# An encoder layer in split float32: residual rows and middle activations kept in DRAM during the FFN, token sums packed, splitting queued part by part

## The chip, the core and the metric

The kernel runs on one core of a Trainium2 chip. The metric is the device time of one execution in microseconds, lower is better; a median of several runs is given, with their lowest and highest. The profile and the trace come from one profiled execution.

The engines are called TensorE (PE in the profile; PEld is its weight load), VectorE (DVE), ScalarE (ACT), GpSimd (POOL) and SyncE (SP). Each works through its own queue in order; semaphores tie the queues together. SyncE's and GpSimd's queues also issue DMAs.

## What is computed

One layer of a bidirectional encoder on 256 tokens with 2048 features, all float32: a layer norm, one input projection, two kinds of attention, an output projection, and then the part that this change touches, a gated feed-forward network of width 5632 between two layer norms.

```python
h = layer_norm(x, ln_in_g, ln_in_b)
proj = einsum('bsd,de->bse', h, w_in)            # ... two attentions -> mixed inputs
mixed = einsum('bse,ed->bsd', concatenate([na_out, diff_out], -1), w_out)
h = layer_norm(ALPHA * h + mixed, ln1_g, ln1_b)
ffn = einsum('bsf,fd->bsd', silu(h @ w_gate) * (h @ w_up), w_down)
h = layer_norm(ALPHA * h + ffn, ln2_g, ln2_b)
```

## The kernel before

**Split products.** Every large product is made of three matmuls on operands in the format fp32r. A float32 matrix is split into a high half (`hi`, a rounding copy, made by ScalarE) and a low half (`lo`, the rest, a subtraction made by VectorE); the product is hi*hi + hi*lo + lo*hi. Weights are split on chip: `load` (line 326) brings a unit, 128 rows by 1024 columns, to `raw[u]` through SyncE's queue; `split_hi` and `split_lo` make `wh[u]` and `wl[u]`.

**Slots.** Nearly all large tiles come from one pool, `slab`, of 46 slots of 4 KB per partition (`slot`, line 262). A new tile takes a slot whose last tenant is done; if its last reader has not finished, the instruction that fills the slot waits. Residual rows `h` (4 slots) live there from the start to the end, the split transposed FFN input `h1T` (8) and the token sums `forms` (8) through the gate/up stage, and the finished middle activations as `mid_whole` (one per 512 columns, 11 in all) from their making to the down projection.

**Units and stages.** `units` lists the weight units in the order of work: w_in, w_out, then one group of 512 columns of gate and up (`f`, units `FFN` to `SG`), then five slices j of 1024 columns, each with 16 gate units and 16 up units (`SG` to `SE`), then the down projection in two halves of 44 units.

**Fast products.** In the five slices two units make a pair: a 2x2 block of weights against a 2x2 block of tokens. Even pairs (`SEVEN`) are done with seven products instead of eight, which needs sums of weight blocks (`seven_parts`, line 891: sums on VectorE, then their splits on both engines) and sums of token blocks (`more_forms`, line 508: four per pair). Odd pairs take eight plain products with two token differences (line 508 too). `take_product` (line 975) issues the three matmuls of a product into one of eight PSUM banks and, after a product's last pair, the operations that combine the products: a copy on ScalarE, then sums on VectorE, and `block_end` (line 1011) with the activation function or the product of gate and up. Of the up half each finished 128x512 block is transposed on TensorE and copied by ScalarE into `mid_whole` (`mid_side`, line 866); `mid_split` (line 874) splits it for the down projection.

**What sets the order.** Instructions are written out in an order found while the program is built. `Timed` (line 60) keeps a model clock for each engine. The loop at line 1254 goes through the TensorE steps; before each it loads units up to `NPRE` or, for products, `NPRE_S` ahead, forces the splits of the next `URGENT` steps, lets `side` tasks (transposes, norms, attention) go where the model has room, and queues splitting work for steps up to `AHEAD` or `AHEAD_S` ahead. For a seven-product pair that work is a list of five stages, each with operations of both engines, and a stage goes out only if both engines' clocks are at most `SPARE` (2 us) beyond TensorE's:

```python
for p in coming:
    todo = prepare(*p)
    while todo and nc.ready(*todo[0][0]) <= now and max(nc.clock["act"], nc.clock["dve"]) <= now + SPARE:
        todo.pop(0)[1]()
    if todo:
        break
```

The model knows when a tile in a ring or a bank is reused, but not when a slot of the slab is.

Of the kernel before, what the change touches and what calls it, by code (L numbers as in the profile page):

```python
# [15 lines left out]
P = 128  # L16
# [18 lines left out]
URGENT = 3  # L35
NSG = 5
SEVEN = (0, 2, 4, 6)


class Engine:  # L40
# [6 lines left out]
    def __getattr__(self, op):  # L47
        def call(*args, **kw):
            result = getattr(self.engine, op)(*args, **kw)  # L49
            outs, ins = [], []  # L50
            for i, (key, x) in enumerate([("", x) for x in args] + list(kw.items())):
                if hasattr(x, "tensor") and hasattr(x, "ap"):
                    (outs if key in ("out", "accum_out") or (i == 0 and not key) else ins).append(x)
            self.timed.note(self.name, op, outs, ins)
            return result

        return call
# [187 lines left out]
def layer_kernel(ctx: ExitStack, tc: tile.TileContext, A: dict, out: bass.AP):  # L245
# [5 lines left out]
    tmp = ctx.enter_context(tc.tile_pool(name="tmp", bufs=2))  # L251
    slab = ctx.enter_context(tc.tile_pool(name="slab", bufs=46))
    dram = ctx.enter_context(tc.tile_pool(name="dram", bufs=1, space=bass.MemoryType.DRAM))
# [4 lines left out]
    def nm(s):  # L258
        uid[0] += 1
        return f"{s}_{uid[0]}"  # L260

    def slot(shape, dt=F32):
        return slab.tile(shape, dt, tag="slab", name=nm("sl"))

# [78 lines left out]

    def split(u):
        if u not in wh:
            split_hi(u)
            split_lo(u)

    acc = {}

    def mm_step(t, u):
# [5 lines left out]
        xh = xh[:, t * P : (t + 1) * P]  # L357
        xl = xl[:, t * P : (t + 1) * P]
# [7 lines left out]
        nc.tensor.matmul(a1, xl, hi[:, 512:], start=False, stop=sp)  # L366

    def mm_step32(t, u, lhs):
# [19 lines left out]
    AHEAD = 7  # L388
    AHEAD_S = 13
    NPRE = 7  # L390
    NPRE_S = 5

# [54 lines left out]
    def ln_side(key, t, g, b, store, tiles, n_whole):  # L447
# [10 lines left out]
        for c in range(4):  # L458
# [46 lines left out]

    hF, forms = {}, {}

    def more_forms(i):
# [16 lines left out]
        f = f[:, :n]  # L525
        parts = slot([P, 2, n, P], F32R)
        yield "act", [f]
# [346 lines left out]
    def mid_split(c):  # L874

        if c not in mid_tiles:
            side.drain_until(lambda: have.get(("mid whole", c), 0) == 2)
            new_T(mid, mid_tiles, c)
            hi, lo = mid_tiles[c]
            nc.scalar.activation(hi, mid_whole[c], AF.Copy)  # L880
            nc.vector.tensor_tensor(lo, mid_whole[c], hi.bitcast(F32), op=ALU.subtract)
            have["mid", c, 0] = have["mid", c, 1] = 1

# [5 lines left out]
    sums = {}  # L889

    def seven_parts(u):

        r1, r2 = raw[u], raw[u + 1]

        def one():
            sums[u] = dict(b11=slot([P, 2, 512], F32R), t=[slot([P, 2, 512]), slot([P, 2, 512])])
            nc.scalar.activation(sums[u]["b11"][:, 0], r1[:, :512], AF.Copy)
            nc.vector.tensor_tensor(sums[u]["t"][0][:, 0], r1[:, :512], r1[:, 512:], op=ALU.add)

        def two():  # L900
            split_hi(u + 1)
            s = sums[u]
            nc.vector.tensor_tensor(s["t"][0][:, 1], r1[:, 512:], r2[:, 512:], op=ALU.add)
            nc.vector.tensor_tensor(s["b11"][:, 1], r1[:, :512], s["b11"][:, 0].bitcast(F32), op=ALU.subtract)

        def three():
            split_lo(u + 1)
            s = sums[u]
            s["hi"] = [slot([P, 2, 512], F32R), slot([P, 2, 512], F32R)]
            s["lo"] = [slot([P, 2, 512], F32R), slot([P, 2, 512], F32R)]  # L910
            nc.scalar.activation(s["hi"][0], s["t"][0], AF.Copy)

        def four():
            s = sums[u]
            a, b = s["t"]
            nc.vector.tensor_tensor(b[:, 0], a[:, 0], r2[:, 512:], op=ALU.add)
            nc.vector.tensor_tensor(b[:, 1], b[:, 0], r2[:, :512], op=ALU.add)
            nc.scalar.activation(s["hi"][1], b, AF.Copy)
            nc.vector.tensor_tensor(s["lo"][0], a, s["hi"][0].bitcast(F32), op=ALU.subtract)

        def five():
            s = sums[u]
            nc.vector.tensor_tensor(s["lo"][1], s["t"][1], s["hi"][1].bitcast(F32), op=ALU.subtract)

        return [([r1], one), ([r1, r2], two), ([r2], three), ([r2], four), ([r2], five)]

# [4 lines left out]
    def products(u):  # L931
# [12 lines left out]

        def t(n, m):
            return lambda: (sums[u]["hi"][n][:, m], sums[u]["lo"][n][:, m])

        a_, b_, c_, d_ = x(0, 0), x(1, 0), x(0, 1), x(1, 1)
        if i in SEVEN:
            def b11():  # L950
                return sums[u]["b11"][:, 0], sums[u]["b11"][:, 1]

            return [
                (1, a_, b11),
                (2, b_, b(1, 0)),
                (3, f(2), b(1, 1)),
                (5, f(3), t(0, 0)),
                (7, f(0), t(0, 1)),
                (6, f(1), t(1, 0)),
                (4, d_, t(1, 1)),  # L960
            ]
# [13 lines left out]
    def take_product(u, n):  # L975
# [10 lines left out]
        nc.tensor.matmul(q[m], xh, yl, start=False, stop=False)  # L986
        nc.tensor.matmul(q[m], xl, yh, start=False, stop=stop)
        if not any(x in left for x in (1, 6, 7)) and 1 in q:
# [4 lines left out]
            nc.vector.tensor_tensor(vw[:, 0], q[7], e[:, 1], op=ALU.add)  # L993
            part["q1"], part["v"], part["vw"], part["w"] = e[:, 0], e[:, 1], vw[:, 0], vw[:, 1]
            for x in (1, 6, 7):
# [11 lines left out]
        elif stop and m == 4:  # L1007
            block_end(name, 1, 0, q[4], part["vw"], ALU.subtract)
            banks.give(q.pop(4))

# [152 lines left out]
    def last_steps():  # L1163
# [6 lines left out]
        for i, a in enumerate(acc[1]):  # L1170
            cols = slice(i * 512, i * 512 + 512)
            for u in us:
                xh, xl = (x[:, P:] for x in mid[units[u]["k"]])
                nc.tensor.matmul(a, xh, wh[u][:, cols], start=False, stop=False)
# [10 lines left out]
    def prepare(u, seven):  # L1185

        if u not in stages:
            if seven:
                stages[u] = seven_parts(u)
            else:  # L1190
                stages[u] = [([raw[u]], lambda: split(u))]
                if units[u]["group"][0] == "d" and isinstance(units[u]["group"], tuple):
                    c = units[u]["k"] // 4
                    if c not in mid_tiles:
                        stages[u].insert(0, ([], lambda: mid_split(c)))
        return stages[u]

    class Step:
# [24 lines left out]
        def finish_parts(self):  # L1223
            for p in self.parts:
                todo = prepare(*p)
                while todo:
                    todo.pop(0)[1]()

        def operands(self):
# [8 lines left out]
            t = self.t  # L1238
            return [wh[self.u], wl[self.u], *(x[:, t * P : (t + 1) * P] for x in un["lhs"][un["k"]])]

# [13 lines left out]
    for i, step in enumerate(order):  # L1254
# [5 lines left out]
        for _ in range(8):  # L1260
            now = nc.clock["pe"]
            side.elementwise(now, BACKLOG)
            for p in coming:
                todo = prepare(*p)
                while todo and nc.ready(*todo[0][0]) <= now and max(nc.clock["act"], nc.clock["dve"]) <= now + SPARE:
                    todo.pop(0)[1]()
                if todo:
                    break
            task, when = side.best()
# [51 lines left out]
```

## Time and profile before

| | us |
|---|---|
| median of 3 runs | 1149.44 |
| lowest, highest | 1146.36, 1149.57 |
| profiled execution, its own time | 1151.8 |
| its span, first to last instruction | 1150.0 |

| engine | busy us | share of the span |
|---|---|---|
| TensorE, matmuls | 1128.6 | 98% |
| TensorE, weight loads | 914.2 | 79% |
| VectorE | 855.2 | 74% |
| ScalarE | 572.3 | 50% |
| GpSimd | 43.2 | 4% |

How to read it: an instruction of the trace has a start and an end on its engine; idle time before it is put down to the instruction that released it last. All operations are recorded under one line (L49, a helper), so groups are told apart by their tiles: `sl` is any tile of the slab, `acc` a PSUM bank, `s`, `o` and `nb` are rings of small tiles, `ident` the matrix for transposes. In a table of stretches the columns are: length, then busy time and count of PE, PEld, DVE, ACT and POOL, the granted clock of TensorE as a share, the DMA engines' busy share, GB/s. The FFN starts near 405 us, the five slices run from about 463 to 904, the down projection from there to 1138.

### The profile page before, as it was taken

To read this page: it belongs to the slowest core of one execution; us is meant where nothing else is said; L and a number is where in the kernel's file an instruction comes from. 1 tells how busy PE (TensorE), PEld (TensorE's weight loads), DVE (VectorE), ACT (ScalarE), POOL (GpSimd) and SP (SyncE) were. 2 spreads that over 40 slices of the span, in tenths; PEclk is the share of its full clock that TensorE was granted. 3 is DMA by queue.
4 is the path that set the end of the run, shared out by engine and by line. 5 is a ranking of instruction groups with operands and counts; after the bars stand their busy time and mean duration, and the time that the engine had idled before them with its cause. 6 is when DMAs were issued, how large, how long until landed. Compare 5 with 4: busy or idle time off the path is not lost.

```text
span 1150.0 us, 13909 instructions
## 1 busy us (share of the span) xinstructions
PE 1128.6 (98%) x5064; PEld 914.2 (79%) x5064; DVE 855.2 (74%) x1110; ACT 572.3 (50%) x740; POOL 43.2 (4%) x81
## 2 busy tenths in 40 slices
PE   9999999999999999999999999999999999999997
PEld 4788888888888858888778778778778888888885
DVE  7863866447784399989999989999989855455535
ACT  5552655426572155654654654555556544434420
POOL 2000002111000000000000000000000000000001
PEclk9999999999999999999999999999999999999999
DMA  9864548796676623656555556465556755577621
GB/s 329 268 187 151 154 148 184 189 216 157 163 255 204 235 91 115 213 187 203 195 185 196 170 188 234 128 220 183 170 196 223 269 194 174 177 232 246 217 79 73
DMA packets 64053, 218.51 MB, mean 190 GB/s; under 512 B 7669, under 2 KB 7797, under 8 KB 63985
## 3 DMA queue, kind: packets, MB, share of 16 engines
q1 hardware_dynamic: 61056, 209.74, 54.3%
q0 software_dynamic: 2768, 7.81, 5.0%
q8 instruction: 39, 0.64, 0.2%
q14 instruction: 30, 0.24, 0.1%
q10 hardware_dynamic: 160, 0.08, 0.0%
HBM read 215.50 MB, written 2.11 MB: 189 GB/s over the span
## 4 chain that ended last, share of the span: by engine, by line
PE 78%; DVE 13%; issue 3%; ACT 3%; DMA 1%; POOL 1%; POOLq 0%; ACTq 0%; DVEq 0%
PE acc L49 78%; DVE sl L49 10%; ACT sl L49 3%; DVE s L49 1%; DVE o L49 1%; ACT s L49 0%; DMA ident<-in_c_ident_dram 0%; DMA sl<-in_w_gate_dram 0%; DMA sl<-in_w_up_dram 0%; DVE stats L49 0%; POOL rstd L49 0%; POOL rs L49 0%; ACT o L49 0%; ACT L49 0%; POOLq L1317 0%
## 5 line engine op out<-in xcount | busy, mean ns | idle before, releaser
L49 PE MATMUL acc<-sl,sl 128*128 128x512 f32 (+1 forms) x4712 | 1076.7, 389 | 12.2 <-DVE o L49 5.5
L49 PEld LDWEIGHTS acc<-sl,sl 128*128 128x128 f32 x4712 | 869.5, 189 | 200.5 <-DVE sl L49 10.8
L49 DVE TENSOR_TENSOR sl<-sl,sl 128x1024 fp32r<-128x1024 f32 (+2 forms) x611 | 628.7, 1073 | 124.9 <-ACT sl L49 96.6
L49 ACT ACTIVATE sl<-sl 128x1024 fp32r<-128x1024 f32 (+1 forms) x491 | 473.2, 1011 | 297.1 <-DVE sl L49 167.5
L49 ACT ACTIVATE sl<-acc 128x256 fp32r<-128x256 f32 (+2 forms) x70 | 33.0, 499 | 102.4 <-PE acc L49 89.7
L49 DVE TENSOR_TENSOR sl<-acc,sl 128x256 fp32r<-128x256 f32 (+2 forms) x92 | 53.2, 593 | 33.4 <-ACT sl L49 32.6
L49 ACT COPY sl<-acc 128x512 f32<-128x512 f32 x50 | 28.2, 586 | 77.5 <-PE acc L49 77.4
L49 DVE SCALAR_TENSOR_TENSOR sl<-sl,acc 128x512 f32<-128x512 f32 x16 | 10.9, 679 | 58.1 <-PE acc L49 58.1
L49 DVE TENSOR_SCALAR sl<-acc 128x512 f32<-128x512 f32 x8 | 5.5, 688 | 37.2 <-PE acc L49 37.2
L49 DVE TENSOR_TENSOR sl<-sl 128x512 f32<-128x512 f32 x40 | 27.3, 683 | 0.0
L49 POOL DMA_DIRECT2D sl<-in_ln_g_dram x4 | 2.2, 560 | 652.2 <-DMA sl<-in_w_down_dram 596.7
L49 POOL DMA_DIRECT2D nb<-in_na_rpb_dram x32 | 19.6, 620 | 87.5 <-DVE s L49 87.5
L49 ACT ACTIVATE s<-s 128x512 f32<-128x512 f32 x20 | 12.3, 633 | 20.6 <-DVE s L49 20.6
L49 ACT ACTIVATE s<-s,mx 128x256 f32<-128x256 f32 x32 | 15.9, 500 | 12.5 <-DVE mx L49 12.5
L49 PEld LDWEIGHTS acc<-ident,s 128*128 128x128 f32 x136 | 17.1, 145 | 4.7 <-DVE o L49 0.9
L49 PE MATMUL acc<-ident,s 128*128 128x128 f32 x136 | 20.7, 281 | 0.1
L49 PEld LDWEIGHTS acc<-ident,sl 128*128 128x128 f32 x128 | 15.0, 140 | 7.0 <-issue 3.2
L49 DVE SCALAR_TENSOR_TENSOR sl<-sl,rstd,sl 128x512 f32<-128x512 f32 x22 | 16.5, 751 | 4.0 <-POOL rstd L49 3.1
L49 DVE BATCH_NORM_STATS2 stats<-sl 128x6 f32<-128x512 f32 x24 | 16.3, 690 | 3.0 <-DMA sl<-in_x_dram 2.4
L49 DVE SCALAR_TENSOR_TENSOR sl<-sl,mv,sl 128x512 f32<-128x512 f32 x24 | 17.7, 746 | 0.3
L49 PE MATMUL acc<-ident,sl 128*128 128x128 f32 x128 | 17.6, 273 | 0.1
L49 ACT ACTIVATE rows<-ident,rstd 128x128 f32<-128x128 f32 x1 | 0.4, 402 | 34.3 <-POOL rstd L49 34.3
(74 smaller groups left out, 198.9 us busy)
## 6 DMA issues: line engine op xcount, KB each, us to landing
sl<-in_w_in_dram SPq DMA_DIRECT2D x96, 512.0 KB, 4.9
sl<-in_w_down_dram SPq DMA_DIRECT2D x88, 512.0 KB, 4.3
sl<-in_w_gate_dram SPq DMA_DIRECT2D x80, 512.0 KB, 4.0
sl<-in_w_up_dram SPq DMA_DIRECT2D x80, 512.0 KB, 4.3
sl<-in_w_out_dram SPq DMA_DIRECT2D x32, 512.0 KB, 5.4
sl<-in_w_gate_dram SPq DMA_DIRECT2D x16, 256.0 KB, 4.0
sl<-in_w_up_dram SPq DMA_DIRECT2D x16, 256.0 KB, 4.2
sl<-in_x_dram SPq DMA_DIRECT2D x8, 256.0 KB, 5.0
```

Of the source, the lines that this page charges most:

```text
L49: result = getattr(self.engine, op)(*args, **kw)
```

## The change

It has three parts.

First, tiles leave the slab during the FFN. The residual rows are written to DRAM (`h_d`) by GpSimd's queue as they are transposed and read back by SyncE's queue ten units before the second half of the down projection. Finished middle activations are copied to a ring of two tiles, written to DRAM (`mid_d`) by GpSimd's queue, and read back chunk by chunk by SyncE's queue when the down projection's units are loaded. The token sums of two plain pairs share one slot.

Second, splitting is cut into single operations, each with its engine, what it reads and which parts must precede it, and `next_part` picks the first one in the window whose own engine has room and whose input is due. Weight sums get their tiles later, and the model is told when slab tiles are given up (`leave`, `slot`).

Third, the window for products grows from 13 to 20 steps and loads from five to eight units ahead.

```diff
+SLOTS = 46
     def slot(shape, dt=F32):
-        return slab.tile(shape, dt, tag="slab", name=nm("sl"))
+        t = slab.tile(shape, dt, tag="slab", name=nm("sl"))
+        if slots["used"] < SLOTS:
+            slots["used"] += 1
+        elif slots["left"]:
+            old = min(slots["left"], key=lambda x: nc.idle(x))
+            slots["left"].remove(old)
+            nc.follows(t, old)
+        return t
+    h_d = dram.tile([2 * P, D], F32, name="h_d")
+    mid_d = dram.tile([NFC * P, 1024], F32, name="mid_d")
     def load(u):
+        if u == U - KF - 10:
+            for t in range(2):
+                h[t] = [slot([P, 1024]) for _ in range(2)]
+                for i in range(2):
+                    nc.sync.dma_start(h[t][i], h_d[t * P : (t + 1) * P, i * 1024 : (i + 1) * 1024])
+        if units[u]["group"] == ("d", 0) and units[u]["k"] % 4 == 0:
+            c = units[u]["k"] // 4
+            side.drain_until(lambda: have.get(("mid whole", c), 0) == 2)
+            mid_whole[c] = slot([P, 2, 4, P])
+            nc.sync.dma_start(mid_whole[c], mid_d[c * P : (c + 1) * P, :])
-    AHEAD_S = 13
+    AHEAD_S = 20
-    NPRE_S = 5
+    NPRE_S = 8
             if key == "1":
+                nc.gpsimd.dma_start(h_d[t * P : (t + 1) * P, c * 512 : (c + 1) * 512], chunk(h[t], c))
+                if c % 2:
+                    leave(h[t][c // 2])
...
-        parts = slot([P, 2, n, P], F32R)
+        if n == 4:
+            parts = slot([P, 2, n, P], F32R)
+        elif len(halves) % 2 == 0:
+            halves.append(slot([P, 2, 2, 2, P], F32R))
+            parts = halves[-1][:, 0]
...
     def mid_side(c, t, m):
         yield "pe", [m]
         bk = pe_transpose4(m)
-        if c not in mid_whole:
-            mid_whole[c] = slot([P, 4, S])
-        nc.scalar.copy(mid_whole[c][:, :, t * P : (t + 1) * P], bk.rearrange("p (a b) -> p a b", b=P))
+        f = ring("nb", 2, (P, 512))
+        nc.scalar.copy(f, bk)
+        nc.gpsimd.dma_start(mid_d[c * P : (c + 1) * P, t * 512 : (t + 1) * 512], f)
...
     def seven_parts(u):
...
+        return [
+            op("act", hi11, lambda: [r1]),
+            op("dve", t1, lambda: [r1]),
+            op("dve", t3, lambda: [r1, r2]),
+            op("act", lambda: split_hi(u + 1), lambda: [r2]),
+            op("dve", lo11, lambda: [s["b11"][:, 0]], (0,)),
+            op("act", hi13, lambda: [s["t"]], (1, 2)),
+            op("dve", t24, lambda: [s["t"]], (1, 2)),
+            op("dve", lo2, lambda: [wh[u + 1]], (3, 6)),
+            op("act", hi24, lambda: [s["u"]], (6,)),
+            op("dve", lo13, lambda: [s["hi"]], (5,)),
+            op("dve", lo24, lambda: [s[2]], (8,)),
+        ]
...
+    def next_part(coming, now):
+        for p in coming:
+            parts = prepare(*p)
+            for o in parts:
+                if o["done"] or not all(parts[i]["done"] for i in o["after"]):
+                    continue
+                clock = nc.clock[o["engine"]]
+                if clock <= now + SPARE and nc.ready(*o["reads"]()) <= max(clock, now):
+                    return o
+        return None
...
-            for p in coming:
-                todo = prepare(*p)
-                while todo and nc.ready(*todo[0][0]) <= now and max(nc.clock["act"], nc.clock["dve"]) <= now + SPARE:
-                    todo.pop(0)[1]()
-                if todo:
-                    break
+            o = next_part(coming, now)
+            while o is not None:
+                emit_part(o)
+                o = next_part(coming, now)
```

## Rows read from the trace of the kernel before

**Rows 1.** Page, section 1: TensorE's busy us, share of the span, instructions.

```profile
PE 1128.6 (98%) x5064; PEld 914.2 (79%) x5064; DVE 855.2 (74%) x1110; ACT 572.3 (50%) x740; POOL 43.2 (4%) x81
```

**Rows 2.** Timeline, PE: start us, us, what, xcount [idle before <-releaser].

```profile
425.93 4.77 PE L49 MATMUL acc<-sl,sl 128*128 128x512 f32 x18 [0.53 <-DVE sl L49]
431.20 29.43 PE L49 MATMUL acc<-sl,sl 128*128 128x512 f32 x127 [0.51 <-DVE sl L49]
...
507.80 37.49 PE L49 MATMUL acc<-sl,sl 128*128 128x512 f32 x164 [0.42 <-DVE sl L49]
...
548.52 1.66 PE L49 MATMUL acc<-sl,sl 128*128 128x512 f32 x6 [0.97 <-DVE o L49]
...
593.80 37.48 PE L49 MATMUL acc<-sl,sl 128*128 128x512 f32 x164 [0.16 <-DVE sl L49]
...
681.43 37.48 PE L49 MATMUL acc<-sl,sl 128*128 128x512 f32 x164 [0.19 <-DVE sl L49]
...
770.38 37.49 PE L49 MATMUL acc<-sl,sl 128*128 128x512 f32 x164 [0.17 <-DVE sl L49]
...
812.10 2.90 PE L49 MATMUL acc<-sl,sl 128*128 128x512 f32 x6 [1.81 <-DVE o L49]
...
859.65 39.15 PE L49 MATMUL acc<-sl,sl 128*128 128x512 f32 x164 [0.77 <-DVE sl L49]
898.64 0.60 PE L49 MATMUL acc<-ident,s 128*128 128x128 f32 x4
898.99 3.02 PE L49 MATMUL acc<-sl,sl 128*128 128x512 f32 x12
901.85 1.04 PE L49 MATMUL acc<-ident,s 128*128 128x128 f32 x8
902.64 1.63 PE L49 MATMUL acc<-sl,sl 128*128 128x512 f32 x6
...
904.46 234.18 PE L49 MATMUL acc<-sl,sl 128*128 128x512 f32 x1032
```

**Rows 3.** Busy time in four slices of the gate/up stage.

```profile
507.80:593.80 86.00, 84.58 (x377) 68.95 (x377) 82.45 (x99) 49.62 (x59) 0.00 (x0) 1.00 0.58 193
593.80:681.40 87.60, 84.86 (x376) 68.94 (x376) 82.49 (x99) 49.46 (x58) 0.00 (x0) 1.00 0.57 197
681.40:770.40 89.00, 86.19 (x377) 70.17 (x377) 82.94 (x99) 49.58 (x59) 0.00 (x0) 0.98 0.54 183
770.40:859.60 89.20, 85.44 (x373) 69.58 (x373) 81.78 (x98) 48.66 (x57) 0.00 (x0) 0.98 0.57 188
```

**Rows 4.** Groups of VectorE, first slice: busy us, mean ns, idle before.

```profile
L49 DVE TENSOR_TENSOR sl<-sl,sl 128x1024 fp32r<-128x1024 f32 x40 | 47.6, 1219 | 1.9 <-ACT sl L49 1.6
```

**Rows 5.** The same groups in the last whole slice, 770.4 to 859.6.

```profile
L49 DVE TENSOR_TENSOR sl<-sl,sl 128x1024 fp32r<-128x1024 f32 x40 | 47.8, 1219 | 3.6 <-ACT sl L49 3.3
L49 DVE TENSOR_TENSOR sl<-sl,sl 128x512 f32<-128x512 f32 x24 | 16.5, 687 | 1.6 <-DMA sl<-in_w_up_dram 1.4
...
L49 DVE TENSOR_TENSOR sl<-acc,sl 128x512 f32<-128x512 f32 x6 | 4.1, 688 | 1.2 <-ACT sl L49 1.0
```

**Rows 6.** Waits of SyncE's queue, 454 to 900: us, times, longest.

```profile
SPq L49 <- PE acc L49: 269.6, 87, 8.2
```

**Rows 7.** Chain that ended last, window 700 to 725.

```profile
699.87 5.92 PE acc L49 x27
705.79 4.07 DMA sl<-in_w_gate_dram
```

**Rows 8.** DMA issues by line: count, KB each, median us to landing.

```profile
nb<-in_na_rpb_dram POOLq DMA_DIRECT2D x32, 64.0 KB, 9.8
...
out_dram<-sl SPq DMA_DIRECT2D x8, 256.0 KB, 2.1
```

**Rows 9.** Timeline, GpSimd, eight bias reads.

```profile
283.61 4.88 POOL L49 DMA_DIRECT2D nb<-in_na_rpb_dram  x8 [42.34 <-DVE s L49]
```

**Rows 10.** Busy time while those eight are issued.

```profile
283.60:288.50 4.90, 4.90 (x29) 4.26 (x28) 3.02 (x9) 3.06 (x7) 4.88 (x8) 1.00 0.86 31
```

More of the change, by code (lines that the diff above doesn't have):

```diff
@@ L260, in nm, with leave @@
         return f"{s}_{uid[0]}"
+    slots = dict(used=0, left=[])
     def slot(shape, dt=F32):
-        return slab.tile(shape, dt, tag="slab", name=nm("sl"))
+        t = slab.tile(shape, dt, tag="slab", name=nm("sl"))
[6 more added lines that the diff above has]
+        return t
+    def leave(*tiles):
+        slots["left"] += tiles
     rings = {}
@@ L342, in split_lo, with tokens @@
         nc.vector.tensor_tensor(wl[u], raw[u], wh[u].bitcast(F32), op=ALU.subtract)
[L344 to L347, printed above, removed]
     acc = {}
+    def tokens(x, t):
+        return x[:, t] if len(x.shape) == 3 else x[:, t * P : (t + 1) * P]
     def mm_step(t, u):
@@ L525, in more_forms @@
         f = f[:, :n]
-        parts = slot([P, 2, n, P], F32R)
+        if n == 4:
[3 more added lines that the diff above has]
+            parts = halves[-1][:, 0]
+        else:
+            parts = halves[-1][:, 1]
+            halves.append(None)
         yield "act", [f]
@@ L889, in layer_kernel, with mid_hi, mid_lo, op @@
-    sums = {}
+    def mid_hi(c):
+        hi, lo = mid_tiles[c] = slot([P, 2, 4, P], F32R), slot([P, 2, 4, P], F32R)
+        nc.scalar.activation(hi, mid_whole[c], AF.Copy)
+    def mid_lo(c):
+        hi, lo = mid_tiles[c]
+        nc.vector.tensor_tensor(lo, mid_whole[c], hi.bitcast(F32), op=ALU.subtract)
+        leave(mid_whole[c])
+        for i in range(4):
+            mid[4 * c + i] = hi[:, :, i, :], lo[:, :, i, :]
+        have["mid", c, 0] = have["mid", c, 1] = 1
+    sums = {}
+    def op(engine, fn, reads=(), after=()):
+        return dict(engine=engine, fn=fn, reads=reads, after=after, done=False)
@@ L891, in seven_parts, with one_parts, lo @@
+    def one_parts(u):
+        def lo():
+            split_lo(u)
+            leave(raw[u])
+        return [op("act", lambda: split_hi(u), lambda: [raw[u]]), op("dve", lo, lambda: [wh[u]], (0,))]
     def seven_parts(u):
         r1, r2 = raw[u], raw[u + 1]
[L895 to L898, printed above, removed]
@@ L913, in four @@
[L913 to L923, printed above, removed]
@@ L925, in seven_parts, with t1, t3, hi11 @@
-        return [([r1], one), ([r1, r2], two), ([r2], three), ([r2], four), ([r2], five)]
+        s = sums[u] = {}
+        def t1():
+            s["t"] = slot([P, 2, 512])
+            nc.vector.tensor_tensor(s["t"][:, 0], r1[:, :512], r1[:, 512:], op=ALU.add)
+        def t3():
+            nc.vector.tensor_tensor(s["t"][:, 1], r1[:, 512:], r2[:, 512:], op=ALU.add)
+        def hi11():
+            s["b11"] = slot([P, 2, 512], F32R)
+            nc.scalar.activation(s["b11"][:, 0], r1[:, :512], AF.Copy)
@@ L987, in take_product @@
         nc.tensor.matmul(q[m], xl, yh, start=False, stop=stop)
+        if n + 1 == len(products(u)):
+            s = sums.get(u)
+            leave(*([wh[u], wl[u]] if s is None else [s["b11"], s["hi"], s["lo"], s[2], s[4]]), wh[u + 1], wl[u + 1])
         if not any(x in left for x in (1, 6, 7)) and 1 in q:
@@ L993, in take_product @@
             nc.vector.tensor_tensor(vw[:, 0], q[7], e[:, 1], op=ALU.add)
+            part["tiles"] = e, vw
             part["q1"], part["v"], part["vw"], part["w"] = e[:, 0], e[:, 1], vw[:, 0], vw[:, 1]
@@ L1008, in take_product @@
             block_end(name, 1, 0, q[4], part["vw"], ALU.subtract)
+            leave(*part["tiles"])
             banks.give(q.pop(4))
@@ L1172, in last_steps @@
             for u in us:
-                xh, xl = (x[:, P:] for x in mid[units[u]["k"]])
+                xh, xl = (tokens(x, 1) for x in mid[units[u]["k"]])
                 nc.tensor.matmul(a, xh, wh[u][:, cols], start=False, stop=False)
@@ L1224, in finish_parts @@
             for p in self.parts:
-                todo = prepare(*p)
-                while todo:
-                    todo.pop(0)[1]()
+                for o in prepare(*p):
+                    if not o["done"]:
+                        emit_part(o)
         def operands(self):
```

78 lines of the change are left out of this document (45 added, 33 removed).

## The prediction

> **What bounds the kernel now.** First the engines' totals [rows 1]: TensorE counts as busy for 98% of the 1150.0 us span, so nothing that leaves its work alone can give much. The reader should distrust that number all the same: a busy TensorE here is one whose matmuls overlap, and small stops hide in it. The change leaves TensorE's instruction list alone (the same products and transposes), so all it can win is time that TensorE loses between matmuls.
>
> So I count that loss by spacing. In the down projection 1032 matmuls run back to back in 234.18 us, and an undisturbed stretch of 164 takes 37.49 us: (234.18 - 37.49) / (1032 - 164) = 0.2266 us each [rows 2]. Transposes cost (1.04 - 0.60) / 4 = 0.11 us each [rows 2]. One slice j of the gate/up stage has 2 x 60 products of three matmuls and 16 transposes: 360 x 0.2266 + 16 x 0.11 = 83.3 us at full pace. The timeline resumes after a stall at the same place of each slice, so differences of those starts are whole slices: 507.80, 593.80, 681.43, 770.38, 859.65 [rows 2]. They are 86.00, 87.63, 88.95 and 89.27 us long, so 2.7, 4.3, 5.6 and 6.0 us are lost, growing. From 859.65 to 904.46, 182 products' matmuls and 16 transposes should take 43.0 us and take 44.8: 1.8 more. Together **20.4 us**. The down projection has no stop in its 1032 matmuls [rows 2], so the gate/up stage is the stock from which the change can win.
>
> What causes it: VectorE is busy 82.5, 82.5, 82.9 and 81.8 us in the four slices [rows 3], against TensorE's 83.3. Two engines with nearly the same work can only both run at full pace if VectorE never waits, and it waits: in the last slice 3.6 us for ScalarE's high halves, 1.6 us for weight rows that had not landed, 1.2 us for ScalarE's copy of the first product; in the first slice the first of these is 1.9 us [rows 4, 5]. One chain shows the mechanism: TensorE works until 705.79, only then can a weight load start (its slot was still being read), it lands 4.07 us later [rows 7], VectorE's sums and splits and then the block ends queue behind it, and TensorE, needing a bank that a block end still reads, stops near 723, as it does for 1.81 us before 812.10 [rows 2]. There six matmuls then take 2.90 us, against 1.66 after the 0.97 us stop at 548.52 [rows 2]; the mean granted clock of the last two slices is 0.98, that of the earlier two 1.00 [rows 3]. A longer stop thus costs about 1.2 us more behind it. The loads' queue spends 269.6 us of this stage waiting for TensorE [rows 6], which has nothing else to give it than a slot that it has stopped reading. That fits the growth: 20 of the 46 slots hold residual rows (4), split FFN input (8) and token sums (8) for the whole stage, and one more is taken per finished 512 columns of middle activations: 1 at the start, 9 in the last slice. What is left falls from 25 to 17. A pair with seven products takes 11 slots from load to last matmul, a plain one 6: 17 slots are one round of two pairs, 15 products or 10.2 us.
>
> **The change, part by part.**
>
> *Slots.* Parking frees 4 for the residual and 1 to 9 for the activations; packing the two-column token sums frees 2. Instead of 25 to 17, 32 slots are left throughout: up to 15 more, 15/17 x 10.2 = 9 us of lead. The deeper settings (loads eight units ahead instead of five, splits 20 products ahead instead of 13) use it: three more raw slots and some seven products' worth, 7/15 x 17 = 8. That makes 11 of the 15, so they fit. A load issued three units or one and a half pairs (7.7 us) earlier covers the 4.07 us of landing [rows 7]. The 1.6 us of waits for loads go.
>
> *Ordering by parts.* The same VectorE and ScalarE instructions, each now queued by itself once its input is due and its own engine is free, where before a stage of a pair went out whole when both engines were. What goes is most of VectorE's wait for high halves (1.9 to 3.6 us a slice [rows 4, 5]). What stays is the wait for the copy of the first product, since copy and subtraction are still issued back to back (1.2 us [rows 5]). VectorE's slice then takes 82.5 + 1.2 = 83.7 us if no wait for high halves is left, and 85.6 if the 1.9 of the first slice stays everywhere. Against 83.3 that leaves TensorE 0.4 to 2.3 us short per slice. I take 1.1, nearer the lower end, because the lead of several pairs absorbs single waits: about **5.5 us** for five slices. The long stops, and with them the clock, should go. What is late next is VectorE itself.
>
> *Residual rows out and back.* Eight issues on GpSimd's queue, the first four while the first 128 rows' norm is transposed, ahead of the second rows' reciprocal root there. An issue holds GpSimd 4.88 / 8 = 0.61 us [rows 9]; four before the root are 2.4 us, ready over some 5 us, so I cost them at nothing; without that cover the second norm is up to 2.4 us late. Coming back they are four loads on SyncE's queue ten units before the second half of the down projection, ahead of weight loads that are seven units early: 0 us, at most one landing (4.07 us [rows 7]).
>
> *Activations out and back.* ScalarE's copy stays, now into a ring of two tiles; each then leaves through GpSimd (20 issues of 0.61 us on an engine otherwise idle there). The added wait: the third copy of a slice must wait until the first has left, and queued behind it on ScalarE are the high halves, which VectorE needs. Transposes of the first and the third tile start 901.85 + 0.44 - 898.64 = 3.65 us apart where nothing stalls [rows 2]. The output rows, also 256 KB from a tile to DRAM but on SyncE's queue, land 2.1 us after their issue [rows 8]; with the issue 2.7 us, so the copy does not wait. The far bound is the bias reads on GpSimd's queue, 9.8 us to landing [rows 8]: then ScalarE stands 9.8 + 0.6 - 3.65 = 6.8 us per slice, with the transposes' bank held as long. I take the write row, the nearest in kind and size. VectorE has not been seen to hold GpSimd up: eight issues took 0.61 us each while VectorE was busy for 3.0 of their 4.9 us [rows 10]. The Trainium skill ("SBUF — State Buffer", section "SBUF: two separate sides") states that a DMA issued from GpSimd cannot have its descriptors written while VectorE holds the port pair that the two share, in the modes that use both ports or, against a GpSimd instruction that reads SBUF, with two SBUF operands. If the writes fell under it, they would be late wherever VectorE works without a pause, and the sum would be that of the third rival below; by the row it is the sum below.
>
> The eleven loads back (0.5 MB each, SyncE's queue) lie in a stage whose TensorE shows no loss: 0 us, at most one landing again. Their splits are the same instructions as before.
>
> *Other stages* use the new ordering too, with the settings of before; I cost it at 0, within 2 us either way: where VectorE splits the norm's output, two stops of 0.53 and 0.51 us [rows 2] could go, or, with two engines queued more eagerly, come again elsewhere.
>
> **Sum.** 20.4 - 5.5 = 14.9 us less. The profiled execution took 1151.8 us (span 1150.0 and 1.8 around it), 2.4 above the median of the runs; I take the difference from the median, 1149.44 - 14.9 = **1134.5 us**.
>
> **Rivals.**
>
> *Only the slots help (1140 to 1146).* VectorE stays short of lead, and every slice behaves like the first, when slots were many: 2.7 us lost in each. Gain 1.6 + 2.9 + 3.3 = 7.8: 1141.6. For it: VectorE's 99% load. Against: the first slice too had late high halves, which the ordering addresses.
>
> *Everything goes (1127 to 1129).* VectorE's lead covers the 0.4 us a slice: 20.4 won, and up to 2 more in other stages: 1149.4 - 20.4 - 2 = 1127. For it: VectorE has a slightly smaller load than TensorE. Against: it has no reserve.
>
> *The parked writes hold ScalarE (slower).* If a write takes longer than 3.65 us from copy to landing, ScalarE stops in every slice and the splits behind it come late. At the far bound, 6.8 us in five slices make 34 us of stop; with the 14.9 won, 1149.4 - 14.9 + 34 = 1168.5. It is slower than before once the stop exceeds 3.0 us a slice, a landing 3.0 + 3.65 - 0.6 = 6.0 us after the issue. For it: GpSimd's reads in the trace land that late [rows 8]. Against: those are strips behind seven others in one burst, the write's row is 2.1 us, and ScalarE is busy for only 49.6 of a slice's 86 us [rows 3], so part of a stop would be made good. The Trainium skill's rule on the shared port pair, named above, would make this the likelier case; no row shows GpSimd's issues in a stage where VectorE is as full as here, which is why it keeps a chance.
>
> *No effect (1146 to 1153).* The slots are taken by other tiles, or the deeper window only queues work that VectorE cannot do sooner.
>
> **How the numbers follow.** Forecast (1129 to 1140) 0.60; only slots (1140 to 1146) 0.14; everything goes 0.09; no effect 0.09; slower 0.08. A measurement can tell some 0.3%, 3.4 us, from no change: faster is 0.60 + 0.14 + 0.09 = 0.83, the same 0.09, slower 0.08. The range 1127 to 1145 takes in the first three.
>
> **What would show it.** Slices of 84 to 85 us in TensorE's timeline, no longer growing; no stop over 1 us at block ends and a granted clock of 1.00; VectorE at 98% or more of a slice and no wait for gate or up rows; copies into the ring not waiting for DMA. Wrong: slices that still grow (slots not the cause), VectorE waiting as long for high halves (order not the cause), ScalarE waiting for parked writes, or a late second norm near 412.

## The result and the profile after

The changed kernel takes 1129.99 us (median of 4 runs, 1129.63 to 1130.14), the kernel before 1149.21 beside it: 0.984 of it, 95% interval 0.982 to 0.986, 19.2 us less. The profiled execution took 1130.1 us with a span of 1128.2, 21.8 below the span of before.

First the totals of the page, busy us and share of the span for each engine:

```profile
PE 1116.9 (99%) x5064; PEld 911.8 (81%) x5064; DVE 848.6 (75%) x1110; ACT 569.9 (51%) x740; POOL 60.3 (5%) x111
```

TensorE has the same 5064 matmuls [rows 1] in 11.7 us less busy time; VectorE and ScalarE have the same number of instructions. GpSimd has 30 more, the writes of parked tiles. Then TensorE's timeline, to be read like [rows 2] (start, length, what, count, idle before):

```profile
426.21 33.16 PE L50 MATMUL acc<-sl,sl 128*128 128x512 f32 x145 [0.57 <-DVE sl L50]
...
462.78 79.83 PE L50 MATMUL acc<-sl,sl 128*128 128x512 f32 x351
...
551.75 73.03 PE L50 MATMUL acc<-sl,sl 128*128 128x512 f32 x321
...
635.26 72.35 PE L50 MATMUL acc<-sl,sl 128*128 128x512 f32 x318
...
721.48 70.31 PE L50 MATMUL acc<-sl,sl 128*128 128x512 f32 x309
...
802.27 73.03 PE L50 MATMUL acc<-sl,sl 128*128 128x512 f32 x321
```

From 462.78 on no row of the gate/up stage has an idle bracket. From 551.75 to 802.27 there are 321 + 318 + 309 matmuls in these long rows, 132 in the short rows between them and 48 transposes: 1080 x 0.2266 + 48 x 0.11 = 250.0 us at full pace, and it took 250.5. So a slice is 83.5 us, against 86.0 to 89.3 [rows 2], and does not grow. One of the two stops near 430 is left (426.21). The table of stretches, for the whole stage (columns as in [rows 3]):

```profile
462.00:885.00 423.00, 423.00 (x1908) 350.37 (x1907) 412.83 (x491) 249.72 (x294) 11.38 (x21) 1.00 0.66 222
```

TensorE is busy without a break at a granted clock of 1.00; in before it was 0.98 in the last two whole slices [rows 3]. VectorE is busy 412.8 of 423 us, 97.6%; up to 881, where its last work of the stage ends, it is 411.7 of 418 us, 98.5%. What VectorE waited for in 463 to 885 us (total us, times, longest), first in the kernel before:

```profile
DVE sl L49 <- ACT sl L49: 18.3, 23, 1.6
DVE sl L49 <- DMA sl<-in_w_up_dram: 2.9, 3, 1.5
DVE sl L49 <- DMA sl<-in_w_gate_dram: 1.1, 1, 1.1
```

and after:

```profile
DVE sl L50 <- PE acc L50: 2.5, 3, 1.1
DVE sl L50 <- ACT sl L50: 1.0, 2, 0.5
```

The waits for ScalarE and for weight rows, 22.3 us, have become 1.0 us. Those for ScalarE are of two kinds: of the 18.3 us, 14.1 stood before subtractions that need a high half and 4.2 before subtractions that need ScalarE's copy of a first product, which this group shows:

```profile
L49 DVE TENSOR_TENSOR sl<-acc,sl 128x512 f32<-128x512 f32 x27 | 18.6, 688 | 4.6 <-ACT sl L49 4.2
```

The 1.0 us left is for high halves alone. The 2.5 us for TensorE stand before operations that read a bank, so VectorE is ahead there and waits for a product.

One wait falls outside this window. At the very end of the stage the last copy into the ring of parked tiles waits 5.1 us for an earlier write, and VectorE, whose splits for the down projection need the high halves queued behind that copy, stands for 8.7 us (881 to 890). TensorE has no stop there: enough splits of the down projection are done.

One reading of before did not hold up: the loads' queue still waits for TensorE, 294.4 us between 463 and 885 against 250.1 before, although no load comes late any more. That loads wait for a slot says nothing of whether they come late.

### The profile page after: what moved, and what is told of

The parts are those of the page before. It is cut to its first block, busy times and chain, and to the rows that moved or that the text cites. A ratio compares the mean times of both kernels' runs of the same rounds, so it can differ in the third digit from the quotient of the medians.

```text
span 1128.2 us, 13969 instructions
## 1 busy us (share of the span) xinstructions
PE 1116.9 (99%) x5064; PEld 911.8 (81%) x5064; DVE 848.6 (75%) x1110; ACT 569.9 (51%) x740; POOL 60.3 (5%) x111
## 4 chain that ended last, share of the span: by engine, by line
PE 95%; DVE 2%; ACT 1%; POOL 1%; DMA 0%; issue 0%; POOLq 0%; ACTq 0%; DVEq 0%
PE acc L50 95%; DVE sl L50 2%; ACT sl L50 0%; DMA ident<-in_c_ident_dram 0%; POOL rs L50 0%; DVE stats L50 0%; POOL rstd L50 0%; DVE s L50 0%; ACT o L50 0%; DVE o L50 0%; ACT L50 0%; POOLq L1420 0%; DVE mv L50 0%; ACT nb L50 0%; ACT rows L50 0%
## 5 line engine op out<-in xcount | busy, mean ns | idle before, releaser
L50 POOL DMA_DIRECT2D mid_d<-nb x22 | 11.9, 542 | 458.4 <-ACT nb L50 458.4
L50 ACT COPY nb<-acc 128x512 f32<-128x512 f32 x24 | 14.1, 589 | 39.6 <-PE acc L50 31.9
L50 ACT COPY sl<-acc 128x512 f32<-128x512 f32 x28 | 15.4, 590 | 32.6 <-PE acc L50 32.5
L50 PE MATMUL acc<-ident,s 128*128 128x128 f32 x136 | 19.8, 272 | 0.0
```

## The experiments

The change was split into three: parking and packing (slots), ordering by parts, and deeper windows. Times are medians; ratios are to the kernel before, timed beside each, with 95% intervals.

| | slots | ordering | windows | us | ratio |
|---|---|---|---|---|---|
| before | - | - | - | 1149.2 | 1 |
| e1 | - | - | yes | 1152.8 | 1.003 (1.002 to 1.004) |
| e2 | yes | - | - | 1146.4 | 0.998 (0.996 to 0.999) |
| e3 | yes | - | yes | 1144.4 | 0.995 (0.993 to 0.997) |
| e5 | - | yes | - | 1138.2 | 0.990 (0.989 to 0.992) |
| e6 | packing only | yes | yes | 1140.7 | 0.993 (0.991 to 0.995) |
| e4 | yes | yes | - | 1133.5 | 0.986 (0.984 to 0.989) |
| after | yes | yes | yes | 1130.0 | 0.984 (0.982 to 0.986) |

**Windows alone (e1).** In the kernel before:

```diff
-    AHEAD_S = 13
+    AHEAD_S = 20
     NPRE = 7
-    NPRE_S = 5
+    NPRE_S = 8
```

> The kernel before with the deeper windows alone (splits 20 products ahead, loads 8 units ahead), nothing parked, whole stages as before. If the slots are the cause, the slots left (25 falling to 17) can't carry the deeper window: the last slices are as long as before or longer (89 us), total 1146 to 1153. If the short window was the cause by itself, slices of 84 to 85 us and 1132 to 1137.

1152.8 us, slower than before. TensorE's timeline at the same place in each slice:

```profile
508.20 37.51 PE L49 MATMUL acc<-sl,sl 128*128 128x512 f32 x164 [0.49 <-DVE sl L49]
...
594.22 37.48 PE L49 MATMUL acc<-sl,sl 128*128 128x512 f32 x164 [0.17 <-DVE sl L49]
...
680.86 37.52 PE L49 MATMUL acc<-sl,sl 128*128 128x512 f32 x164 [0.17 <-DVE sl L49]
...
768.79 39.05 PE L49 MATMUL acc<-sl,sl 128*128 128x512 f32 x164 [0.17 <-DVE sl L49]
...
860.87 39.08 PE L49 MATMUL acc<-sl,sl 128*128 128x512 f32 x164 [0.76 <-DVE sl L49]
```

The slices are 86.0, 86.6, 87.9 and 92.1 us. Looking further ahead with the same slots makes the two middle ones 1.0 us shorter and the last 2.8 us longer than before [rows 2]: the growth that was put down to slots comes later and steeper.

**Slots alone (e2).** `h_d`, `mid_d`, their loads and the packed sums in the kernel before; its whole stages and windows stay.

```diff
+                nc.gpsimd.dma_start(h_d[t * P : (t + 1) * P, c * 512 : (c + 1) * 512], chunk(h[t], c))
...
+        f = ring("nb", 2, (P, 512))
+        nc.scalar.copy(f, bk)
+        nc.gpsimd.dma_start(mid_d[c * P : (c + 1) * P, t * 512 : (t + 1) * 512], f)
```

> The kernel before with parking and packing alone, old windows, whole stages. If the slots are the cause of the growth, all slices become like the first of before (86 us, 2.7 lost each): 1140 to 1143. If the order or the window is the cause, no change: 1146 to 1152. If parked writes cost time in themselves, slower than before.

1146.4 us: by its time at the edge of the second theory, that slots change nothing. But the slices tell what slots do:

```profile
593.62 37.48 PE L49 MATMUL acc<-sl,sl 128*128 128x512 f32 x164 [0.16 <-DVE sl L49]
...
681.08 37.47 PE L49 MATMUL acc<-sl,sl 128*128 128x512 f32 x164 [0.17 <-DVE sl L49]
...
768.20 37.48 PE L49 MATMUL acc<-sl,sl 128*128 128x512 f32 x164 [0.17 <-DVE sl L49]
...
855.30 36.80 PE L49 MATMUL acc<-sl,sl 128*128 128x512 f32 x161 [0.17 <-DVE sl L49]
```

87.46, 87.12 and 87.10 us: alike, none growing. The slots were the cause of the growth, as predicted, and with room VectorE waits no more for weight rows; the loss common to these slices, 3.8 us each against 83.3 at full pace, stays. It is larger than the 2.7 of the first slice of before [rows 2], so the gain was less than forecast; why it is larger stays open.

**Slots and windows (e3).** Both edits above together.

> Parking, packing and deeper windows in the kernel before, with the old whole stages. If the ordering by parts only adds the last bit, 1131 to 1136 and slices of 84. If it is what lets VectorE run without waits, VectorE still waits about 2 us a slice for high halves and the total is 1139 to 1143.

1144.4 us, a little above the second range. With slots the same deeper windows help, by 2.0 us. VectorE's waits for ScalarE are still there (463 to 885):

```profile
DVE sl L49 <- ACT sl L49: 15.4, 20, 1.7
```

Of these, 11.2 us are for high halves and 4.2 for the copy of a first product. Where they arise is seen in the timelines of ScalarE and VectorE (a high half, and the subtraction that needs it):

```profile
500.60 1.04 ACT L49 ACTIVATE sl<-sl 128x1024 fp32r<-128x1024 f32 x1
501.68 1.23 DVE L49 TENSOR_TENSOR sl<-sl,sl 128x1024 fp32r<-128x1024 f32 x1 [1.65 <-ACT sl L49]
```

So room and depth together leave 14 us of the change's gain to the ordering.

**Old windows (e4).** The changed kernel with 13 products and 5 units.

```diff
-    AHEAD_S = 20
+    AHEAD_S = 13
     NPRE = 7
-    NPRE_S = 8
+    NPRE_S = 5
```

> The changed kernel with the old windows (13 products, 5 units). If depth is needed for the last slices, some stops of TensorE come back: 1134 to 1142. If the ordering by parts with free slots suffices, 1130 to 1132.

1133.5 us, between the two ranges and 3.5 more than the full change. Two stops of TensorE came back, of 0.9 us each (673 to 675 and 842 to 844). VectorE waits 5.7 us for ScalarE instead of 1.0.

**Ordering alone (e5).** The changed kernel with residual rows and middle activations in the slab, unpacked sums and the old windows.

```diff
-        f = ring("nb", 2, (P, 512))
-        nc.scalar.copy(f, bk)
-        nc.gpsimd.dma_start(mid_d[c * P : (c + 1) * P, t * 512 : (t + 1) * 512], f)
+        if c not in mid_whole:
+            mid_whole[c] = slot([P, 2, 4, P])
+        nc.scalar.copy(mid_whole[c][:, t], bk.rearrange("p (a b) -> p a b", b=P))
```

> The ordering by parts alone: nothing parked or packed, old windows. If ordering is the larger cause and slots the smaller, about 1137 to 1142 with slices that still grow as slots fill up; if ordering alone takes nearly all, 1133 to 1135; if the slots are needed for it to work at all, above 1144.

1138.2 us: 11.0 of the 19.2 come from ordering by itself. The first two slices run without a stop of TensorE; long ones come late in the stage, as slots fill (1.46 us at 711.65, 1.97 at 798.61). VectorE waits for weight rows again, once for 2.4 us before 700 us and then, from 700 to 885:

```profile
DVE sl L50 <- DMA sl<-in_w_gate_dram: 2.9, 4, 1.8
DVE sl L50 <- ACT sl L50: 2.6, 3, 1.9
DVE sl L50 <- DMA sl<-in_w_up_dram: 1.9, 2, 1.3
```

**Ordering and windows (e6).** As e5 with the deep windows and the packed sums. Deep windows with unpacked sums and nothing parked were not tried.

> The changed kernel with residual rows and middle activations kept in the slab; sums stay packed, windows stay deep. Slots left fall from 27 to 19 through the stage. If parking matters, the first slices are free of stops and the last two lose 2 to 4 us each: 1134 to 1140. If it does not matter, 1129 to 1131.

1140.7 us, slower than e5 although its windows are deeper. Stops begin in the third slice:

```profile
710.70 0.65 PE L50 MATMUL acc<-ident,s 128*128 128x128 f32 x4 [0.77 <-DVE s L50]
...
796.67 0.66 PE L50 MATMUL acc<-ident,s 128*128 128x128 f32 x4 [1.45 <-DVE s L50]
```

and from 700 to 885 us VectorE itself stands waiting for TensorE to give up a slot:

```profile
DVE sl L50 <- PE acc L50: 6.4, 6, 2.2
```

In the changed kernel the same line stands before operations that read a bank; here 5.8 of the 6.4 us stand before operations that read slab tiles alone, so it is the slot that they lack, and it ends with TensorE waiting for VectorE. Deeper windows cost about 3 us without room (e1 against before; e6 against e5, though e6 has two slots more by packing) and gain 2 to 3.5 with it (e3 against e2, after against e4).

**What in the ordering does it (e7, e9, e12).** The new ordering does four things at once: it cuts stages into single operations, takes any part that is due, goes by each engine's own clock, and lets the model know when slots are reused. First only the list's order (e7):

```diff
-                if o["done"] or not all(parts[i]["done"] for i in o["after"]):
+                if o["done"]:
                     continue
                 clock = nc.clock[o["engine"]]
                 if clock <= now + SPARE and nc.ready(*o["reads"]()) <= max(clock, now):
                     return o
+                return None
```

> The changed kernel, but parts are queued strictly in their list's order: the first part that is not yet due holds back all later ones. If picking whatever is due is what keeps VectorE filled, its waits for high halves come back and the total is 1136 to 1145. If cutting the stages into single parts with their own engine's clock suffices, 1130 to 1132.

1131.3 us, and no stop of TensorE in the stage. Then the joint clock of before (e9):

```diff
-                clock = nc.clock[o["engine"]]
+                clock = max(nc.clock["act"], nc.clock["dve"])
```

> The changed kernel, but a part goes out only when both engines' model clocks are within 2 us of TensorE's, as before. If cutting the stages into single parts is what fills VectorE, 1130 to 1132, as with the strict order. If it is that each engine goes by its own clock, VectorE's waits for high halves return (1 to 2 us a slice) and the total is 1135 to 1143.

1130.5 us, half a microsecond from the changed kernel. Then all of it undone except the cut (e12), both edits above and:

```diff
-            nc.follows(t, old)
+            del old
...
-                if clock <= now + SPARE and nc.ready(*o["reads"]()) <= max(clock, now):
+                if clock <= now + SPARE and (o["after"] or nc.ready(*o["reads"]()) <= now):
```

> Parking and deep windows as in the changed kernel, with only the cut into single parts kept of the new ordering: parts go out strictly in their list's order, only when both engines' model clocks allow, with a look at the raw rows alone (not at whether a high half is due), and the model does not know when slots are reused. If the cut is what matters, 1130 to 1133, as with the strict order or the joint clock alone. If the model's knowledge of due inputs and slots is what matters, 1138 to 1144, as with whole stages.

1131.3 us, again without a stop of TensorE in the stage. VectorE's waits for ScalarE in 463 to 885:

```profile
DVE sl L50 <- ACT sl L50: 2.6, 4, 0.9
```

That is for high halves, where whole stages in e3, with the same slots and windows, had 11.2; for copies of a first product it waits 0 instead of 4.2. The cut into single operations, with its list, is worth 13.1 us; choosing among parts, separate clocks and the slot model together at most 1.3, too little to tell from nothing. In a whole stage an operation of VectorE goes out right behind the ScalarE operation whose result it needs and waits for it; cut, it can go out later, with other operations of VectorE between.

The list also moves the two sums for products 2 and 4 ahead of a subtraction that waits for ScalarE and makes the sums' tiles later, and no run takes these apart from the cut. But e3's trace speaks for the cut. By the order of VectorE's queue all 11.2 us stand before subtractions of units of plain pairs, as in the lines shown for e3: their stage was a high half and the subtraction that needs it, and there the cut alone is new. The subtractions of seven-product pairs, where list and tiles differ too, did not wait for ScalarE in e3.

**VectorE's reserve (e8).** The first weight sum made twice in each seven-product pair:

```diff
             nc.vector.tensor_tensor(s["t"][:, 0], r1[:, :512], r1[:, 512:], op=ALU.add)
+            if units[u]["k"] // 2 in (0, 2, 4, 6):
+                nc.vector.tensor_tensor(s["t"][:, 0], r1[:, :512], r1[:, 512:], op=ALU.add)
```

> The changed kernel with the first weight sum of every seven-product pair made twice: 40 more VectorE operations of 0.61 us, 4.8 us a slice. VectorE then needs 82.5 + 4.8 = 87.3 us a slice against TensorE's 83.3. If VectorE is the next bound with nearly no reserve, the total grows by about 24 - 5 = 15 to 20 us (1145 to 1150). If it has a reserve of several us a slice, by less than 8.

1148.6 us, 18.6 more for 40 x 0.61 = 24 us of added work (0.61 us is the spacing of such operations back to back; each lasts 0.69, and their ends overlap). In the stage:

```profile
463.00:900.00 437.00, 426.49 (x1886) 347.51 (x1884) 432.31 (x526) 245.86 (x293) 10.29 (x19) 0.99 0.63 212
```

VectorE is busy 432.3 of 437 us (98.9%) and TensorE waits. So VectorE is the next bound, with an estimated 24 - 18.6, some 6 us, of reserve over the stage.

**One tile for parked activations (e10).** The copies of all finished blocks share one tile.

```diff
+    mid_buf = []
...
-        f = ring("nb", 2, (P, 512))
+        if not mid_buf:
+            mid_buf.append(ring("nb", 2, (P, 512)))
+        f = mid_buf[0]
```

> The changed kernel with one tile instead of a ring of two for parked activations: every copy waits until the write before it has landed (0.5 us issue and 4.6 us landing in the changed kernel), while finished tiles come 2.5 to 3.5 us apart, so ScalarE stops some 2 us three times a slice, and the bank is held as long. If a stopped ScalarE costs the time of the stop, as in the prediction's third rival, about 6 us a slice, 1150 to 1160. If its slack and VectorE's lead cover it, 1130 to 1133.

1134.1 us, a little above the second range. ScalarE's waits for the parked writes from 454 to 904 us, which holds all 22 copies, first in the changed kernel and then here:

```profile
ACT nb L50 <- DMA mid_d<-nb: 6.6, 3, 5.1
ACT nb L50 <- DMA mid_d<-nb: 26.4, 9, 6.7
```

TensorE's waits for the copies (none in the changed kernel's stage):

```profile
PE acc L50 <- ACT nb L50: 2.3, 3, 0.8
```

19.8 us more of stop on ScalarE cost 4.1 us. The mechanism of the third rival is real, but about four fifths of it are covered.

**A sum on GpSimd (e11).** Could GpSimd, nearly idle, take work from VectorE?

```diff
-            nc.vector.tensor_tensor(s["t"][:, 0], r1[:, :512], r1[:, 512:], op=ALU.add)
+            nc.gpsimd.tensor_tensor(s["t"][:, 0], r1[:, :512], r1[:, 512:], op=ALU.add)
...
-            op("dve", t1, lambda: [r1]),
+            op("pool", t1, lambda: [r1]),
```

> The changed kernel with the first weight sum of each seven-product pair on GpSimd instead of VectorE: 40 operations of 0.61 us less for VectorE, 24 us over the stage. If the two engines don't disturb each other, VectorE's operations keep their lengths (1.22 us for 1024 columns, 0.69 for 512), its busy time in the stage falls from 412 to about 388 us, and the total stays at 1129 to 1131, since TensorE has no stop left there. If they contend for a shared port, VectorE's operations get longer by some of GpSimd's and the total rises by up to 20 us.

1141.4 us, 11.4 slower. VectorE's groups from 463 to 885 us in the changed kernel (busy, mean ns, idle before):

```profile
L50 DVE TENSOR_TENSOR sl<-sl,sl 128x1024 fp32r<-128x1024 f32 x207 | 239.1, 1219 | 1.0 <-ACT sl L50 1.0
L50 DVE TENSOR_TENSOR sl<-sl,sl 128x512 f32<-128x512 f32 x117 | 80.5, 689 | 1.3
L50 DVE TENSOR_TENSOR sl<-sl,sl 128x512 fp32r<-128x512 f32 x39 | 26.8, 688 | 0.0
...
L50 DVE TENSOR_TENSOR sl<-acc,sl 128x512 f32<-128x512 f32 x30 | 20.6, 688 | 2.8 <-PE acc L50 2.5
```

and with the sum on GpSimd, and then GpSimd's own:

```profile
L50 DVE TENSOR_TENSOR sl<-sl,sl 128x1024 fp32r<-128x1024 f32 x204 | 250.1, 1287 | 0.0
L50 DVE TENSOR_TENSOR sl<-sl,sl 128x512 f32<-128x512 f32 x116 | 101.2, 875 | 1.4
L50 DVE TENSOR_TENSOR sl<-sl,sl 128x512 fp32r<-128x512 f32 x39 | 29.7, 761 | 0.0
L50 DVE TENSOR_TENSOR sl<-acc,sl 128x512 f32<-128x512 f32 x29 | 19.8, 683 | 0.3
```

```profile
L50 POOL TENSOR_TENSOR sl<-sl 128x512 f32<-128x512 f32 x38 | 63.4, 1667 | 249.2 <-PE acc L50 151.0 <-DVE sl L50 79.5 <-ACT s L50 8.9
L50 POOL DMA_DIRECT2D mid_d<-nb x18 | 9.9, 549 | 80.8 <-ACT nb L50 80.8
```

Operations that read two slab tiles grew from 1219 to 1287 ns, from 689 to 875 and from 688 to 761 on average. That is 204 x 68 + 116 x 186 + 39 x 73 ns = 38 us more, against 38 x 0.61 = 23 us saved. The growth lies where the two engines meet: by their times in the trace 79 of these operations run beside an addition of GpSimd and take 1.82, 1.18 and 1.04 us on average, the others 1.21, 0.68 and 0.68. Operations with one operand in PSUM kept their length (688 to 683 ns), but that shows nothing of a shared port: none of them ran beside an addition. The DMA issues on GpSimd kept theirs (542 ns in the changed kernel, 549 here).

No kernel was faster than the changed one; e9 is within half a microsecond of it.

## Why the prediction held, and where its terms were off

**Stock: right.** The loss between matmuls was counted as 20.4 us, and it is gone. From 463.35 to the start of the down projection at 904.46 TensorE takes 441.1 us before, for 1812 matmuls; after it takes 419.5 (462.78 to 882.32) for the last 1809 of them. For the same work that is 20.9 of the 21.8 us by which the spans differ, and the stop that went near 431 gives another 0.5. The count left out some 0.7 us lost between 463.35 and 507.80, where 193 matmuls take 44.45 us instead of 43.7; the changed kernel in turn still loses a little. The medians differ by less, 19.2 us, because the profiled execution of before lay 2.4 us above the median that the prediction subtracted from.

**Remainder: the term that was mis-sized.** 5.5 us were kept for VectorE waits that "stay", 1.1 a slice; 0.2 a slice are left by the count above. (The waits read for it, 1.9 us in the first slice and 3.6 and 1.2 in the last, are all the idle time before those operations; what ScalarE ended is 1.6, 3.3 and 1.0 of it [rows 4, 5].) The failed step is that VectorE must wait for ScalarE's copy of the first product because the two are issued back to back. They still are, but VectorE now has other operations queued ahead of the subtraction, so the copy is done when it comes there. An example (ScalarE's copy, then VectorE's sums and, behind them, the subtraction that needs the copy):

```profile
495.13 0.57 ACT L50 COPY sl<-acc 128x512 f32<-128x512 f32 x1
490.53 7.16 DVE L50 TENSOR_TENSOR sl<-sl,sl 128x512 f32<-128x512 f32 x8
497.61 1.41 DVE L50 TENSOR_TENSOR sl<-acc,sl 128x512 f32<-128x512 f32 x2
```

The copy ends 1.9 us before the subtraction starts. Waits for it were 4.2 us in before, 4.2 with room and depth but whole stages (e3), and are 0 in the changed kernel and with the cut alone (e12). So the second rival (everything goes) came closest by mechanism. Its time without the 2 us for other stages is 1149.4 - 20.4 = 1129.0; the measured 1130.0 lies between that and the forecast of 1134.5, at the low end of the forecast's range.

That the sum came within 4.5 us is in part luck: of the 14.9 us, 7.8 were put down to slots and 7.1 were left for ordering and windows, and these two shares were wrong in opposite directions, as follows.

**Slots: mechanism right, share too large.** They caused the growth: with room and nothing else the slices are alike (e2), without room late stops come back even with the new ordering (e5, e6). The share forecast for them alone, 7.8 us, came out as 2.8. The step that failed took the first slice's 2.7 us as what remains when room is given; 3.8 a slice remained.

**Ordering: the larger part.** It was expected to take the waits for high halves, and does; it gives 11 us alone and 14 with slots and windows, and with the windows 16.4 on top of the slots (after against e2), where the sum left 7.1 for both. Of the reason given, that each operation is queued by itself once its input is due and its own engine is free, the first half is enough (e12): with the joint clock, or without asking whether a high half is due, the time is within 1.3 us of the changed kernel (e9, e12).

**Deeper windows fit, as counted,** and need the slots: negative without, positive with them.

**Parked rows: cost nothing, though landings were underestimated.** Count, KB, median us from issue to landing:

```profile
mid_d<-nb POOLq DMA_DIRECT2D x22, 256.0 KB, 4.6
sl<-mid_d SPq DMA_DIRECT2D x11, 512.0 KB, 5.6
...
h_d<-sl POOLq DMA_DIRECT2D x8, 256.0 KB, 3.5
```

4.6 us for a parked block, more than twice the 2.1 of the output rows [rows 8] that were taken for it, and within the far bound of 9.8. By the prediction's own sum, 0.6 + 4.6 against 3.65 us between the first and third copy, ScalarE would stop 1.5 us a slice. Up to 885 us it stopped

```profile
ACT nb L50 <- DMA mid_d<-nb: 1.5, 2, 1.3
```

in all, because finished blocks now come further apart: in the first slice their transposes start at 542.45, 544.97, 548.18 and 551.40 us, the third 5.7 behind the first. In the last slice the third and the fourth come together and the fourth copy, which the prediction's sum left out, waits for the second write:

```profile
888.28 0.59 ACT L50 COPY nb<-acc 128x512 f32<-128x512 f32 x1 [5.09 <-DMA mid_d<-nb]
```

That is the rival's mechanism, once, at a place where splits already done cover it. The rival stayed away for the spacing and the lead and not for the short landing on which the prediction relied.

The second norm's root was not delayed: 9.57 us after the first, as before (9.56). GpSimd's timeline shows one parked write before it and the next ones only behind it, not the four that the prediction put ahead:

```profile
404.91 0.62 POOL L50 DMA_DIRECT2D h_d<-sl  x1 [1.08 <-DVE sl L50]
412.00 0.74 POOL L50 TENSOR_SCALAR rstd<-mv 128x1 f32<-128x1 f32 x1 [6.47 <-DVE mv L50]
...
413.37 2.22 POOL L50 DMA_DIRECT2D h_d<-sl  x4
```

**GpSimd beside VectorE.** The prediction's rival of slow writes was weighed by a rule of the shared port. The Trainium skill ("SBUF — State Buffer", section "SBUF: two separate sides") states that GpSimd and VectorE lock each other out of a shared port pair, where VectorE is in a mode that uses both ports or has two SBUF operands against a GpSimd instruction that reads SBUF. For the writes no run here shows such a lock: each issue held GpSimd 0.54 us, and 11 of the 22 lay wholly beside operations of VectorE that read two slab tiles. Nor did VectorE make the landings late: the three writes that went out while it stood idle, from 881 to 890 us, landed after 6.96, 6.26 and 4.91 us, above the median. So the prediction's step by which the rule made late writes the likelier case does not come out of the trace. For GpSimd's arithmetic the trace agrees with the rule: in e11 VectorE's operations with two SBUF operands stretch where they run beside an addition. That operations with an operand in PSUM do not is not shown.

## What to carry to other kernels

Where two engines have nearly the same work, count the loss by the spacing of the bound engine's instructions, not by its idle column, and then look at what the other one waits for in its own queue: an operation queued right behind the one that feeds it turns into a wait, and cutting the work so that something else can stand between was worth more here than room or depth. Depth without buffers cost time; buffers without depth and order gave little; try them together and take each away once. A wait in a load queue does not show that loads are late, so judge loads by what waits for their data.

## What the runs showed of the hardware

- GpSimd adding two 128x512 float32 halves takes 1.67 us beside a busy VectorE and lengthens VectorE's operations on two SBUF tiles by some 38 us / 38 = 1.0 us per GpSimd operation (e11).
- Issuing a 256 KB write from GpSimd holds it 0.54 us in the same stage, and the block lands after 4.6 us in the median (2.3 to 7.0; changed kernel).
- After a stop of 1.81 us the next six matmuls took 2.90 us instead of 1.66 [rows 2], at a granted clock of 0.50, the lower of TensorE's two levels (1.2 instead of 2.4 GHz; 812.3 to 815.5 in before); the mean of the slice fell to 0.98 [rows 3]. After the stops of 0.97 and 0.96 us at 548.52 and 634.52 it stayed at 1.00. In the changed kernel the whole stage is at 1.00.
